# Three float32r products per weight block, or one plain float32 product on two halves of the array

## The chip, the cores and the metric

One core of one Trainium2 chip runs the whole program in one launch. The metric is the device time of an execution in microseconds; the kernel before takes 2727.23 us (median of three runs, 2720.29 to 2727.84). Inputs, outputs and arithmetic are float32.

## The reference

Two layers of a trunk over 512 latent tokens with 256 context tokens in front, width 1024. Each layer is: half-step SwiGLU, token mixing, half-step SwiGLU, each behind an RMS norm modulated by shift and scale from a conditioning vector.

```python
def half_ffn(h, g, shift, scale, gate, w_gu, w_down):
    return h + 0.5 * gate * swiglu(norm_mod(h, g, shift, scale), w_gu, w_down)   # 1024 -> 2 x 2816 -> 1024
# even layer: [windowed GQA with sink | chunked gMLP spatial gating]; odd layer: [multi-scale pooling | 2-D neighbourhood attention]
y = jnp.concatenate([window_gqa(q, k, v, kc, vc, sink), chunk_gmlp(bu, bv, v_gain, ws, bias)], axis=-1) @ w_out
y = jnp.concatenate([multiscale_pool(xp, w_pool, c_scale), neighbourhood_attn(q, k, v, kc, vc, rpb)], axis=-1) @ w_out
```

The context needs no last half step, so three half steps run over 768 tokens and the fourth over 512. The output is the latent stream (1, 512, 1024).

## The kernel before, in words

The stream `h` lies in SBUF with channels on partitions, in 8 chunks of 128 (`KC`), tokens in the free dimension. Tokens come in groups: `XG` (512 latents), `CG` (256 context tokens), and at the end of the odd mixer `X0` and `X1` (256 latents each). A weight block is 128 rows by 128 columns; a dense product takes a block as the stationary operand and 512 or 256 tokens as the moving one. Per half step there are 22 chunks of the inner dimension (`NFF`), each with 8 gate blocks, 8 up blocks and 8 down blocks, so 528 blocks; the even mixer has 112 blocks in and 64 out, the odd one 128 in (64 of them, pool input and queries, for the latents alone) and 64 out.

Every dense operand is split in two float32r parts, high and low. `chain` (L515) and `out_block` (L529) multiply a block in three products: high by high, high by low, low by high. So do the attention scores (`scores`, L1196 and L1563) and the pooling product (`pooling`, L1647). The parts are made by other engines: weights by `Stream` (L354), which loads 512 KB units into three raw tiles on SyncE's queue, copies the high part (`do_split`) and subtracts the low part (`low`); the modulated input by `modulate` (L581, `second` and `third`); the SwiGLU activations by `hilo` (L348); queries and keys by `headnorm` (L1148); the mixers' outputs by their own copies and subtractions.

Some products are plain float32 already: the attention values (`values`, L1249 and L1603), where each key tile is two calls, one per head of a pair, on 64 columns of the array each, with outputs in the two halves of the partitions; the spatial gating (L1301), in the same form; the modulation vectors (`Ada.job`, L716, and `first_mods`, L970), on 32 columns in four ranges; small sums over partitions (`blk2`, `ones`). Transposes by the identity are float32 on all 128 columns.

The order of the work is written out by the program itself. `Machine` and `Engine.cost` (L64, L155) keep a model of the engines' clocks; `Sched` (L198) holds lanes of background steps (attention, softmax, norms, modulation, gating) and `tick`, called after each dense block, emits those whose operands the model says are ready. `wait_for` (L282) emits background steps alone until a condition holds. The half steps run `ffn_plan` (L447): gate and up of each chunk, and after every second chunk the down product of two chunks. The mixers run `EV_PLAN` and `OD_PLAN` (L298, L300).

The lines of `Engine.cost` that price a TensorE product:

```python
if ins[0].dtype == F32R:
    return n / 2.4 + 2.5
# beside a product on the first columns of the array, those on other columns cost little
if Machine.free(ins[0]) < 128:
    return n / 0.6 + 10.0 if out.offset < out.ap[0][0] else 32.0
return max(n / 0.6, 168.0)
```

Of the kernel before, what the change touches and what calls it, by code (L numbers as in the profile page):

```python
# [8 lines left out]
F32R = mybir.dt.float32r  # L9
# [4 lines left out]
D = 1024  # L14
# [15 lines left out]
LEADS = [400.0, 600.0]  # L30

# Shape-only constants, one row of columns per partition.
# [31 lines left out]
class Machine:  # L64
    """The operations on their way to the engines, with a model of the engines' clocks beside them:
    when an engine gets to an operation, and when its result is there. The order of emission rests on it."""

    # from one engine's result to another's start
# [19 lines left out]
    def rows(self, ap):  # L88
        """What is known of the memory behind an access, and the access's extent."""
# [61 lines left out]
class Engine:  # L151
# [3 lines left out]
    def cost(self, eng, op, out, ins):  # L155
# [42 lines left out]
class Sched:  # L198
    """Emits background steps between the dense matrix products, when the model has their operands ready."""
# [51 lines left out]
    def tick(self, lanes="nmstabg", hooks=True):  # L251
# [7 lines left out]
        for _ in range(40):  # L259
            # what is ready first goes first  # L260
# [21 lines left out]
    def wait_for(self, cond):  # L282
        """Background steps alone, until it holds."""
# [12 lines left out]
# The order of the mixers' dense products: projections by their outputs' names, parts of the way out with the parts they  # L296
# take ("o:" all tokens, "x:"/"c:" latents/context, "0:"/"1:" halves of the latents).
# [6 lines left out]
def trunk(ctx, tc, t, out, stop=None, dbg=None):  # L304
# [5 lines left out]
    rawp = ctx.enter_context(tc.tile_pool(name="rawp", bufs=3))  # L310
# [22 lines left out]
    def copy(out, in_):  # L333
        """By the engine that has it done first."""
# [5 lines left out]
    def minus(out, a, b):  # L340
        """By VectorE or GpSimd, which has it done first."""
        n = Machine.free(out)
        if max(nc.t["dve"], sch.now) + 1.04 * n > max(nc.t["pool"], sch.now) + 2.2 * n + 200.0:
            nc.gpsimd.tensor_tensor(out=out, in0=a, in1=b, op=ALU.subtract)
        else:
            nc.vector.tensor_sub(out, a, b)

    def hilo(hi, lo, src):  # L348
        """Two float32r parts; the lower one when VectorE has time."""
        copy(hi, src)  # L350
        sch.later(sch.at([hi], slack=100.0, eng="dve", lead=300.0), lambda: nc.vector.tensor_sub(lo, src, hi.bitcast(F32)))

# [1 line left out]
    class Stream:  # L354
        def __init__(self):
            self.units = []
            self.dma = self.split = self.taken = 0
            self.raw, self.w, self.low = {}, {}, {}
            self.Q, self.ahead = 3, 3
            # (a room, the units from which on it is no longer there)  # L360
            self.free = [([main.tile([128, D], F32R, name=f"w{i}{p}") for p in "hl"], None) for i in range(4)]
            self.ends, self.long, self.upto = {}, set(), None

        def lend(self, rooms, units):
            """More rooms, of use to the next units only."""
            self.free += [(w, self.taken + units) for w in rooms]

        def room(self, i):
            self.free = [f for f in self.free if f[1] is None or i < f[1]]
            # what stays long goes to a lent room, for the others to have the lasting ones  # L370
            lent = [f for f in self.free if (f[1] is not None) == (i in self.long)]
            return (lent or self.free or [None])[0]

        def pump(self):
            while self.dma < (len(self.units) if self.upto is None else self.upto) and self.dma < min([self.split, *self.low]) + self.Q:
                raw = rawp.tile([128, D], F32, tag="raw", name="raw")
                for dst, src in self.units[self.dma]:
                    nc.sync.dma_start(out=dst(raw), in_=src)
                self.raw[self.dma] = raw
                self.dma += 1  # L380
            i = self.split
            if i < self.dma and i < self.taken + self.ahead:
                r = self.room(i)
                if (r is not None and nc.after([self.raw[i]], [r[0][0]]) <= sch.now
                        and min(nc.t["act"], nc.t["dve"]) <= sch.now + 200.0):
                    self.do_split()

        def do_split(self):
            i = self.split
            raw = self.raw.pop(i)  # L390
            r = self.room(i)
            assert r is not None, i
            self.free.remove(r)
            w, self.ends[id(r[0])] = r
            copy(w[0], raw)
            self.w[i] = w
            self.split += 1

            def low():
                if i in self.low:  # L400
                    self.low.pop(i)
                    if max(nc.t["dve"], sch.now) > max(nc.t["pool"], sch.now) + 1500.0:
                        nc.gpsimd.tensor_tensor(out=w[1], in0=raw, in1=w[0].bitcast(F32), op=ALU.subtract)
                    else:
                        nc.vector.tensor_sub(w[1], raw, w[0].bitcast(F32))
            self.low[i] = low
            sch.later(lambda: max(nc.after([w[0]], []), min(nc.t["dve"], nc.t["pool"] + 1500.0) - 200.0), low)

        def take(self):
            i = self.taken  # L410
            self.taken += 1
            self.pump()
            while self.split <= i:
                self.do_split()
                self.pump()
            if i in self.low:
                self.low[i]()
            return self.w.pop(i)

        def release(self, *ws):  # L420
            self.free += [(w, self.ends[id(w)]) for w in ws]
            self.pump()

    stream = Stream()
    sch.hooks.append(stream.pump)
# [5 lines left out]
    def cols2_unit(w, c0, c1):  # L431
        u = []
        for i, c in enumerate((c0, c1)):
            src = w[:, c:c + 64].rearrange("(k p) f -> p k f", p=128)
            u.append((lambda r, i=i: r.rearrange("p (k f) -> p k f", k=KC)[:, :, 64 * i:64 * i + 64], src))
        return u

    def rows_unit(w, r0):
        return [(lambda r: r, w[r0:r0 + 128, :])]

    def rows2_unit(w, r0, r1):
        return [(lambda r: r[0:64], w[r0:r0 + 64, :]), (lambda r: r[64:128], w[r1:r1 + 64, :])]

    DOWN_BLOCKS = [[2 * i, 2 * i + 1] for i in range(NFF // 2)]

    # a block of the down product comes one chunk after its last part is there
    def ffn_plan(both, first=False):  # L447
        plan = []
        for c in range(NFF):
            plan.append(("gu", c))  # L450
            if c >= 2 and c % 2 == 0:
                plan.append(("down", c // 2 - 1))
        if first:
            # for the gate to get ready
            plan[3:5] = plan[4:2:-1]
        plan.append(("down", NFF // 2 - 1))
        if both:
            # the latents run ahead at the end, so that their norm has the context's products to hide behind
# [1349 lines left out]
```

## Time and profile before

| | |
|---|---|
| timed runs, us | 2727.84, 2727.23, 2720.29 |
| span of the profiled execution, us | 2725.2 |
| its time beyond the span | not on the page; the median is 2.0 us above the span |
| PE busy, share of the span | 2655.8 us, 97% |
| DVE, ACT, POOL busy | 1711.8, 744.4, 683.8 us |
| DMA | 249.31 MB, mean 91 GB/s |
| stages, us from the start | first half step to 617, even mixer to 936, two half steps to 2088, odd mixer to 2350, last half step to the end |

Busy time of PE is the union of its matmul records; since matmuls are pipelined, one record lasts longer than the distance to the next start, so pace is read from starts and not from durations. A record is one executed instruction, and one call in the program can be more than one record. PEclk is the granted clock as a share of 2.4 GHz.

### The profile page before, as it was taken

The numbers are of one execution on the slowest core, as the hardware profiler recorded it, in microseconds if no ns is written. First come the engines' busy times: TensorE is split into PE (matmuls) and PEld (weight loads), VectorE is DVE, ScalarE is ACT, GpSimd is POOL, SyncE is SP. The second block draws the span as 40 slices with busy tenths as digits, with TensorE's granted clock in tenths as the row PEclk, the third lists the DMA queues.
The fourth block names the chain that finished last, engine by engine and source line by source line (L and its number), as shares of the span: only waits on it lengthen the run. The fifth ranks groups of instructions, "written<-read, shape, count | busy, mean of one in ns | idle before, by whom it ended". The sixth has DMA issues, their size and how long they took to land.

```text
span 2725.2 us, 37838 instructions
## 1 busy us (share of the span) xinstructions
PE 2655.8 (97%) x15678; PEld 2284.7 (84%) x15678; DVE 1711.8 (63%) x2459; ACT 744.4 (27%) x1195; POOL 683.8 (25%) x440
## 2 busy tenths in 40 slices
PE   7999999999999889999999999999999999899999
PEld 5888888888888778888888888888888887888887
DVE  6787885456676677788784545444456657644554
ACT  4332331124434432323321411111114333311111
POOL 2453540013433333434440200000003443200000
PEclk9999999999999899999999999999999999899999
DMA  9443532222111144434432122222221212133332
GB/s 271 141 147 124 160 127 62 70 55 72 32 42 34 31 147 147 147 125 145 152 114 70 39 63 64 66 61 74 63 62 52 69 47 64 59 99 93 93 93 85
DMA packets 286918, 249.31 MB, mean 91 GB/s; under 512 B 26178, under 2 KB 256026, under 8 KB 286746
## 3 DMA queue, kind: packets, MB, share of 16 engines
q1 hardware_dynamic: 286378, 246.81, 30.1%
q8 instruction: 123, 2.02, 0.3%
q14 instruction: 49, 0.40, 0.0%
q10 hardware_dynamic: 176, 0.07, 0.0%
q0 software_dynamic: 192, 0.01, 0.0%
HBM read 244.73 MB, written 2.13 MB: 91 GB/s over the span
## 4 chain that ended last, share of the span: by engine, by line
PE 90%; DVE 5%; issue 2%; ACT 1%; POOL 1%; DMA 1%; SPq 0%; ACTq 0%; DVEq 0%; POOLq 0%
PE gb L194 47%; PE bank_c L194 13%; PE bank_d L194 13%; PE bank_e L194 9%; PE bank_f L194 3%; PE S L194 2%; DVE a L194 1%; PE Sx L194 1%; DVE zl L194 1%; PE TB L194 1%; POOL aacc L194 0%; DVE h L194 0%; DMA araw<-in_ada_w 0%; DVE w L194 0%; DMA alent<-in_ada_w 0%
## 5 line engine op out<-in xcount | busy, mean ns | idle before, releaser
L194 DVE TENSOR_TENSOR a<-sg,gb 128x512 f32<-128x512 f32 (+1 forms) x151 | 85.7, 567 | 522.0 <-PE gb L194 521.5
L194 POOL TENSOR_TENSOR aacc<-aacc,amul 128x1024 f32<-128x1024 f32 x112 | 303.6, 2711 | 308.0 <-ACT amul L194 308.0
L194 DVE SCALAR_TENSOR_TENSOR aacc<-araw,st,aacc 128x1024 f32<-128x1024 f32 x112 | 230.8, 2061 | 3.4 <-DMA araw<-in_ada_w 1.5
L194 POOL TENSOR_TENSOR acc<-acc,sq 128x512 f32<-128x512 f32 (+1 forms) x24 | 25.8, 1075 | 780.4 <-ACT sq L194 779.2
L194 PE MATMUL gb<-zl,w0h 128*128 128x512 f32 (+1 forms) x600 | 207.0, 345 | 3.3 <-DVE zl L194 3.2
L194 PE MATMUL gb<-zh,w1h 128*128 128x512 f32 (+1 forms) x608 | 210.1, 346 | 0.0
L194 PE MATMUL gb<-zl,w1h 128*128 128x512 f32 (+1 forms) x608 | 209.0, 344 | 0.0
L194 PE MATMUL gb<-zh,w1l 128*128 128x512 f32 (+1 forms) x608 | 208.8, 343 | 0.0
L194 PE MATMUL gb<-zh,w0h 128*128 128x512 f32 (+1 forms) x600 | 207.9, 347 | 0.0
L194 PE MATMUL gb<-zh,w0l 128*128 128x512 f32 (+1 forms) x600 | 206.2, 344 | 0.0
L194 ACT CAST a<-a 128x512 fp32r<-128x512 f32 (+1 forms) x152 | 80.2, 527 | 460.7 <-DVE a L194 460.4
L194 DVE SCALAR_TENSOR_TENSOR h<-bank_c,mod,h 128x512 f32<-128x512 f32 (+1 forms) x240 | 152.3, 635 | 72.3 <-PE bank_c L194 72.3
L194 PE MATMUL gb<-zh,w3h 128*128 128x512 f32 (+1 forms) x576 | 197.7, 343 | 0.0
L194 PE MATMUL gb<-zl,w3h 128*128 128x512 f32 (+1 forms) x576 | 197.3, 343 | 0.0
L194 PE MATMUL gb<-zh,w3l 128*128 128x512 f32 (+1 forms) x576 | 197.2, 342 | 0.0
L194 DVE SCALAR_TENSOR_TENSOR h<-bank_d,mod,h 128x512 f32<-128x512 f32 (+1 forms) x237 | 150.5, 635 | 70.4 <-PE bank_d L194 70.0
L194 ACT ACTIVATE sg<-gb 128x512 f32<-128x512 f32 (+1 forms) x151 | 75.6, 500 | 418.7 <-PE gb L194 418.7
L194 PE MATMUL gb<-zh,w2h 128*128 128x512 f32 (+1 forms) x536 | 185.1, 345 | 0.0
L194 PE MATMUL gb<-zl,w2h 128*128 128x512 f32 (+1 forms) x536 | 184.1, 344 | 0.0
L194 PE MATMUL gb<-zh,w2l 128*128 128x512 f32 (+1 forms) x536 | 184.0, 343 | 0.0
L194 ACT ACTIVATE amul<-araw,st 128x1024 f32<-128x1024 f32 x112 | 128.8, 1150 | 149.8 <-POOL aacc L194 128.5
L194 DVE TENSOR_TENSOR a<-a,a 128x512 fp32r<-128x512 f32 (+1 forms) x156 | 126.7, 819 | 43.9 <-ACT a L194 43.7
(558 smaller groups left out, 6758.7 us busy)
## 6 DMA issues: line engine op xcount, KB each, us to landing
raw<-in_ffn_w_gu SPq DMA_DIRECT2D x176, 512.0 KB, 4.6
araw<-in_ada_w SPq DMA_DIRECT2D x134, 512.0 KB, 4.0
raw<-in_ffn_w_down SPq DMA_DIRECT2D x88, 512.0 KB, 3.8
raw<-in_od_w_in SPq DMA_DIRECT2D x16, 512.0 KB, 4.1
raw<-in_ev_w_in SPq DMA_DIRECT2D x10, 512.0 KB, 3.7
raw<-in_od_w_out SPq DMA_DIRECT2D x8, 512.0 KB, 3.6
xt<-in_ada_w SPq DMA_DIRECT2D x6, 512.0 KB, 7.2
xt<-in_x SPq DMA_DIRECT2D x4, 512.0 KB, 5.3
```

The source lines that it names most:

```text
L194: return real(*args, **kw)
```

## The change

All float32r parts go. The modulated input is one tile `z`, the SwiGLU activations one value per element, queries and keys `qf` and `kf`, the mixer's slots plain float32 tiles. A dense block is multiplied by `mm`: two plain float32 products, on the first and the last 64 columns of the block, with outputs in the two halves of the partitions and the same moving operand. The scores and the pooling product go the same way. `Stream` loads 1 MB units (two chunks' columns, or two row blocks) straight into seven rooms, with no raw tile and no split. The down product takes four chunks at a time in place of two. `Engine.cost` has other prices for products. The plans of the mixers, `ADA_GAP`, softmax, values, spatial gating and the modulation vectors stay as they are.

```diff
-            if ins[0].dtype == F32R:
-                return n / 2.4 + 2.5
-            # beside a product on the first columns of the array, those on other columns cost little
             if Machine.free(ins[0]) < 128:
-                return n / 0.6 + 10.0 if out.offset < out.ap[0][0] else 32.0
-            return max(n / 0.6, 168.0)
+                return n / 1.2 + 4.0 if out.offset < out.ap[0][0] else 6.0
+            return max(n / 0.6, 112.0)
...
+    def mm(ps, w, z, start, stop):
+
+        for x in range(2):
+            wx = w[x] if isinstance(w, tuple) else w[:, 64 * x:64 * x + 64]
+            nc.tensor.matmul(ps[64 * x:64 * x + 64], wx, z, start=start, stop=stop)
...
     def cols_unit(w, c0):
-        src = w[:, c0:c0 + 128].rearrange("(k p) f -> p k f", p=128)
-        return [(lambda r: r.rearrange("p (k f) -> p k f", k=KC), src)]
+        return [(by_k, w[:, c0:c0 + 256].rearrange("(k p) f -> p k f", p=128))]
...
-            wh, wl = [p[:, 128 * k:128 * k + 128] for p in w]
-            zs = slice(t0, t0 + n)
-            nc.tensor.matmul(ps, wh, zh[:, k, zs], start=(k == 0), stop=False)
-            nc.tensor.matmul(ps, wh, zl[:, k, zs], start=False, stop=False)
-            nc.tensor.matmul(ps, wl, zh[:, k, zs], start=False, stop=(k == KC - 1))
+            mm(ps, w[k], z[:, k, t0:t0 + n], k == 0, k == KC - 1)
             sch.tick()
...
-                        wh, wl = [p[:, 128 * d:128 * d + 128] for p in units[i]]
-                        nc.tensor.matmul(room[d], wh, slots[i][:, 0, zs], start=(i == 0), stop=False)
-                        nc.tensor.matmul(room[d], wh, slots[i][:, 1, zs], start=False, stop=False)
-                        nc.tensor.matmul(room[d], wl, slots[i][:, 0, zs], start=False, stop=(i == nb - 1))
+                        mm(room[d], units[i][:, 128 * d:128 * d + 128], slots[i][:, zs], i == 0, i == nb - 1)
...
-            nc.vector.tensor_tensor(out=a32, in0=sg, in1=ru, op=ALU.mult)
-            hilo(a[:, 0, ts], a[:, 1, ts], a32)
+            nc.vector.tensor_tensor(out=a, in0=sg, in1=ru, op=ALU.mult)
...
-                    for qa, ka in ((0, 0), (0, 1), (1, 0)):
-                        nc.tensor.matmul(S[:, o:o + n], q[rows, qa, qs], khl[rows, ka, kk:kk + n],
-                                         start=(qa + ka == 0), stop=(qa == 1))
+                    mm(S[:, o:o + n], q[rows, qs], kf[rows, kk:kk + n], True, True)
```

## Rows read from the trace of the kernel before

**Rows 1.** The page, part 1: busy time, share of the span, instructions.
```profile
PE 2655.8 (97%) x15678; PEld 2284.7 (84%) x15678; DVE 1711.8 (63%) x2459; ACT 744.4 (27%) x1195; POOL 683.8 (25%) x440
```
**Rows 2.** The chain that ended last, shares of the span by line.
```profile
PE gb L194 47%; PE bank_c L194 13%; PE bank_d L194 13%; PE bank_e L194 9%; PE bank_f L194 3%; PE S L194 2%; DVE a L194 1%; PE Sx L194 1%; DVE zl L194 1%; PE TB L194 1%; POOL aacc L194 0%; DVE h L194 0%; DMA araw<-in_ada_w 0%; DVE w L194 0%; DMA alent<-in_ada_w 0%
```
**Rows 3.** Windows, PE alone: stretch, busy (records), granted clock, DMA share, GB/s.
```profile
1599.37:1649.35 49.98, 49.98 (x289) 1.00 0.22 64
```
**Rows 4.** Timeline of PE, dense products: start, us, instruction, rows*columns, output.
```profile
1650.80 0.39 PE L194 MATMUL gb<-zl,w3h 128*128 128x512 f32 x1
...
1651.93 0.39 PE L194 MATMUL gb<-zh,w3h 128*128 128x512 f32 x1
...
1660.68 0.28 PE L194 MATMUL gb<-zh,w3l 128*128 128x256 f32 x1
...
1661.88 0.28 PE L194 MATMUL gb<-zh,w3h 128*128 128x256 f32 x1
```
**Rows 5.** The odd mixer's value products: the group, and their stretches on the timeline.
```profile
L194 PE MATMUL bank_f<-opT,ovnat 128*64 128x128 f32 x256 | 17.9, 280 | 0.0
...
2143.47 1.09 PE L194 MATMUL bank_f<-opT,ovnat 128*64 128x128 f32 x16
2144.50 0.39 PE L194 MATMUL bank_d<-zh,w1h 128*128 128x256 f32 x1
...
2167.55 0.44 PE L194 MATMUL bank_f<-opT,ovnat 128*64 128x128 f32 x4
2167.92 1.05 PE L194 MATMUL bank_e<-blk,w 128*128 128x2 f32 x8
2168.90 0.88 PE L194 MATMUL bank_f<-opT,ovnat 128*64 128x128 f32 x12
2169.71 0.39 PE L194 MATMUL bank_d<-zh,w3h 128*128 128x256 f32 x1
```
**Rows 6.** The modulation products on 32 columns: the group, and one stretch by start.
```profile
L194 PE MATMUL bank_f<-aacc,pick 128*32 128x256 f32 x256 | 18.0, 401 | 7.3 <-issue 7.3
...
98.22 0.61 PE L194 MATMUL bank_f<-aacc,pick 128*32 128x256 f32 x8
...
98.66 0.40 PE L194 MATMUL bank_f<-aacc,pick 128*32 128x256 f32 x4
```
**Rows 7.** The scores of one item and head: a stretch on the timeline.
```profile
2165.74 0.97 PE L194 MATMUL Sx<-okhl,oqhl 64*128 64x256 f32 x6
2166.64 0.39 PE L194 MATMUL bank_d<-zh,w3h 128*128 128x256 f32 x1
```
**Rows 8.** Transposes on all columns: one group, and two stretches on the timeline.
```profile
L194 PE MATMUL TB<-ident,p 128*128 128x128 f32 x128 | 19.9, 278 | 0.7 <-POOL p L194 0.7
...
2142.89 0.66 PE L194 MATMUL bank_e<-ident,rwx 128*128 128x128 f32 x4
...
2144.96 0.49 PE L194 MATMUL bank_e<-ident,rwx 128*128 128x128 f32 x3
2145.20 0.36 PE L194 MATMUL bank_d<-zh,w1h 128*128 128x256 f32 x1
```
**Rows 9.** What PE waited for: us in total, times, longest us.
```profile
PE bank_c L194 <- DVE zl L194: 5.1, 5, 1.7
PE gb L194 <- ACT a L194: 5.0, 3, 1.7
...
PE bank_c L194 <- DVE h L194: 4.5, 3, 1.8
PE bank_d L194 <- DVE h L194: 4.0, 4, 1.6
```
**Rows 10.** Windows of the mixers: stretch, busy (instructions) of PE, PEld, DVE, ACT, POOL.
```profile
616.80:936.20 319.40, 309.78 (x2108) 258.85 (x2107) 213.96 (x450) 126.94 (x260) 110.91 (x107) 0.99 0.15 40
2088.20:2350.20 262.00, 253.45 (x1653) 212.25 (x1652) 169.05 (x362) 93.33 (x193) 106.66 (x110) 0.99 0.21 58
```
**Rows 11.** One of the four groups that make the weights' low parts on VectorE.
```profile
L194 DVE TENSOR_TENSOR w0l<-raw,w0h 128x1024 fp32r<-128x1024 f32 x72 | 105.3, 1462 | 0.4
```

More of the change, by code (lines that the diff above doesn't have):

```diff
@@ L354, in trunk @@
     class Stream:
         def __init__(self):
[L356 to L372, printed above, removed]
-        def pump(self):
[L375 to L379, printed above, removed]
-                self.dma += 1
[L381 to L407, printed above, removed]
@@ L409, in take @@
-        def take(self):
-            i = self.taken
-            self.taken += 1
-            self.pump()
-            while self.split <= i:
-                self.do_split()
-                self.pump()
[L416 to L422, printed above, removed]
-    stream = Stream()
-    sch.hooks.append(stream.pump)
+            self.keys, self.dmas, self.uses, self.rooms = [], {}, {}, {}
@@ new lines, in __init__, with plan @@
+            self.dma = 0
+            self.free = [main.tile([128, 2 * D], F32, name=f"w{i}") for i in range(ROOMS)]
+            self.upto = None
+        def plan(self, key, dmas):
+            if key not in self.uses:
+                self.keys.append(key)
+                self.dmas[key], self.uses[key] = dmas, 0
+            self.uses[key] += 1
+        def pump(self):
+            while self.free and self.dma < (len(self.keys) if self.upto is None else self.upto):
+                room = min(self.free, key=lambda r: nc.after([], [r]))
+                self.free = [r for r in self.free if r is not room]
+                key = self.keys[self.dma]
+                for dst, src in self.dmas[key]:
+                    nc.sync.dma_start(out=dst(room), in_=src)
+                self.rooms[key] = room
+                self.dma += 1
@@ new lines, in there, with get, release, by_k @@
+        def there(self, key):
+            return key in self.rooms
+        def get(self, key):
+            self.pump()
+            assert key in self.rooms, key
+            return self.rooms[key]
+        def release(self, key):
+            self.uses[key] -= 1
+            if not self.uses[key]:
+                self.free.append(self.rooms.pop(key))
+                self.pump()
+    stream = Stream()
+    def by_k(r):
+        return r.rearrange("p (k f) -> p k f", k=KC)
+    def part(r, i):
+        return [by_k(r)[:, k, 128 * i:128 * i + 128] for k in range(KC)]
@@ L436, in cols2_unit @@
-        return u
[L438 to L447, printed above, removed]
+        for i, rs in enumerate(rows):
+            n = 128 // len(rs)
+            for x, r0 in enumerate(rs):
+                u.append((lambda r, i=i, x=x, n=n: r[n * x:n * x + n, D * i:D * i + D], w[r0:r0 + n, :]))
@@ L448, in ffn_plan @@
+        return u
+    BLOCKS = [list(range(i, min(i + 4, NFF))) for i in range(0, NFF, 4)]
+    def ffn_plan(both):
         plan = []
@@ L450, in ffn_plan @@
             plan.append(("gu", c))
[L451 to L456, printed above, removed]
+            if c >= 4 and c % 4 == 0:
+                plan.append(("down", c // 4 - 1))
+        plan.append(("down", len(BLOCKS) - 1))
         if both:
-            a, b, d = NFF - 2, NFF - 1, NFF // 2 - 1
+            a, b, d = NFF - 2, NFF - 1, len(BLOCKS) - 1
             plan[-4:] = [("gux", a), ("down", d - 1), ("gux", b), ("downx", d), ("guc", a), ("guc", b), ("downc", d)]
@@ new lines, in mixer_units @@
+        for s in plan:
+            if s[1:2] == ":":
+                rows = []
+                for x in s[2:].split(","):
+                    j = int(x[1])
+                    if even:
+                        rows.append((64 * j, 64 * j + 256) if x[0] == "a" else (512 + 128 * j,))
+                    else:
+                        rows.append(((512 if x[0] == "a" else 0) + 128 * j,))
+                stream.plan(("e" if even else "o", s[2:]), parts_unit(w_out, rows))
+                continue
+            for x in s.split(","):
+                key, i = mix_key(even, x)
+                if key[1] == "kv":
+                    u = cols_unit(w_in, 512)
+                elif even and key[1] == "q":
+                    u = cols2_unit(w_in, 128 * key[2], 128 * key[2] + 256)
+                elif even:
+                    u = cols_unit(w_in, {"bu": 768, "bv": 1280}[key[1]] + 256 * key[2])
+                else:
+                    u = cols_unit(w_in, {"p": 0, "q": 512, "k": 1024, "v": 1536}[key[1]] + 256 * key[2])
+                stream.plan(key, u)
@@ L502, in trunk, with weights @@
+    def weights(even, s):
+        key, i = mix_key(even, s)
+        r = stream.get(key)
+        return halves(r, i) if even and key[1] == "q" else part(r, i)
     ffn_units(0, 0)
@@ L527, in soonest, with out_block @@
         return min(banks, key=lambda b: nc.after([], [b]))[:, 0:n]
-    def out_block(slots, units, li, vec, groups, banks, final=None, release=True, quiet=False, ready=None):
+    def out_block(slots, units, li, vec, groups, banks, final=None, quiet=False, ready=None):
         nb, step = len(slots), len(banks) - 1
@@ L794, in gu @@
                 chain(ru, wu, grp)
-            nc.vector.tensor_tensor(out=a32, in0=sg, in1=ru, op=ALU.mult)
-            hilo(a[:, 0, ts], a[:, 1, ts], a32)
-        both, kept, cd = len(groups) == 2, {}, (bank_c, bank_d)
-        plan = ffn_plan(both, (li, fi) == (0, 0))
+            nc.vector.tensor_tensor(out=a, in0=sg, in1=ru, op=ALU.mult)
+        both, cd = len(groups) == 2, (bank_c, bank_d)
+        plan = ffn_plan(both)
         if early is not None:
@@ L826, in ffn, with gu_weights, gu_release, ffn_early @@
                     sch.wait_for(lambda: sch.done(gated))
-                if kind in ("down", "downx"):
-                    us = [stream.take() for _ in DOWN_BLOCKS[i]]
-                part = {"down": groups, "downx": groups[:1], "downc": groups[1:]}[kind]
-                last = i == len(DOWN_BLOCKS) - 1
-                banks = tuple(gb[0:3]) if kind == "downc" else cd + (gb[0], gb[1]) if last else cd + (bank_e,)
-                out_block([slots[cc % 4] for cc in DOWN_BLOCKS[i]], us, li, gate, part, banks, final if last else None,
-                          kind != "downx", not last)
-    def ffn_early(norm, chunks, grps):
-        ws = [(stream.take(), stream.take()) for _ in range(chunks)]
+                us = []
+                for p in BLOCKS[i][::2]:
+                    r = stream.get((li, fi, "d", p))
+                    us += [r[:, 0:D], r[:, D:2 * D]]
+                part_ = {"down": groups, "downx": groups[:1], "downc": groups[1:]}[kind]
+                last = i == len(BLOCKS) - 1
+                banks = tuple(gb[0:3]) if kind == "downc" else cd + (gb[0], gb[1]) if last else cd + (bank_e,)
+                out_block([slots[cc % 6] for cc in BLOCKS[i]], us, li, gate, part_, banks, final if last else None, not last)
+                for p in BLOCKS[i][::2]:
+                    stream.release((li, fi, "d", p))
+    def gu_weights(li, fi, c):
+        return [part(stream.get((li, fi, x, c // 2)), c % 2) for x in "gu"]
+    def gu_release(li, fi, c):
+        for x in "gu":
+            stream.release((li, fi, x, c // 2))
+    def ffn_early(li, fi, norm, chunks, grps):
+        ws = [gu_weights(li, fi, c) for c in range(chunks)]
         n = grps[0][1]
@@ L951, in enter @@
             for b in range(2):
[L952 removed]
+                room = gb[2 + b if i >= 4 else (2 * i + b) % 4]
                 yield sch.at([raw], [room])
@@ L1036, in trunk @@
         sch.add("t", more_loads())
-        zh, zl = [main.tile([128, KC, T], F32R, tag=x, name=x) for x in ("zh", "zl")]
+        z = main.tile([128, KC, T], F32, name="z")
         rooms = {(0, 0): (gb[0], gb[1]), (0, TX): (gb[2][:, 0:TC], gb[3][:, 0:TC]),
@@ L1046, in side_by_side @@
                 sch.tick()
-                if stream.split > len(ws) < 4:
-                    ws.append(stream.take())
+                while len(ws) < 4 and stream.there((0, 0, "gu"[len(ws) % 2], 0)):
+                    ws.append(part(stream.get((0, 0, "gu"[len(ws) % 2], 0)), len(ws) // 2))
                 best, when = None, sch.now + 500.0
@@ L1067, in side_by_side @@
                     sums.remove(best)
-                    for key in ((c, t0), (c, i, "w")):
-                        ends[key] = ends.get(key, 0) + 1
-                    if ends[c, i, "w"] == 2:
-                        stream.release(ws[2 * c + i])
+                    ends[c, t0] = ends.get((c, t0), 0) + 1
                     if ends[c, t0] == 2:
@@ L1074, in side_by_side @@
                         gu(c, None, None, best[3], rooms[c, t0])
+            for c in range(2):
+                gu_release(0, 0, c)
             return 2
@@ L1084, in trunk @@
             return
-        kvq = [stream.take() for _ in range(3)]
+        kvq = [weights(True, x) for x in ("k", "v", "q0")]
         for room, w in zip((bank_c, bank_d, bank_e), kvq):
@@ L1107, in trunk @@
             nc.sync.dma_start(out=gbias[64 * hf:64 * hf + 64], in_=bsrc)
-        slots = [mp.tile([128, 2, T], F32R, name=f"ms{i}") for i in range(4)]
-        khl = mp.tile([128, 2, T], F32R, name="khl")
-        qhl = [mp.tile([128, 2, T], F32R, name=f"qhl{i}") for i in range(2)]
+        slots = [mp.tile([128, T], F32, name=f"ms{i}") for i in range(4)]
+        kf = mp.tile([128, T], F32, name="kf")
+        qf = [mp.tile([128, T], F32, name=f"qf{i}") for i in range(2)]
         vnat = mp.tile([128, 6, 128], F32, name="vnat")
@@ L1132, in kind_of, with proj @@
             return "x" if grp[1] == TX else "c"
-        def proj(w, groups, after, release=True, rooms=(bank_c, bank_d)):
+        def proj(s, groups, after, rooms=(bank_c, bank_d)):
+            w = weights(even, s)
             for grp in groups:
@@ L1162, in headnorm @@
                                   r[:, :2 * nt].rearrange("p (a o) -> p a o", o=1).to_broadcast([128, 2 * nt, 64]))
+            to = dst[:, t0:t0 + n]
+            if not rope:
+                yield from gate(before)
             yield sch.at([rbc[:, :n]], [M])
@@ L1175, in headnorm @@
                 yield sch.at([qn], slack=100.0)
-                nc.vector.tensor_tensor(out=qn, in0=qn, in1=sw, op=ALU.add)
-            yield from gate(before)
-            copy(dst[:, 0, t0:t0 + n], qn)
-            yield sch.at([dst[:, 0, t0:t0 + n]], slack=100.0)
-            nc.vector.tensor_sub(dst[:, 1, t0:t0 + n], qn, dst[:, 0, t0:t0 + n].bitcast(F32))
+                yield from gate(before)
+                nc.vector.tensor_tensor(out=to, in0=qn, in1=sw, op=ALU.add)
         def vtrans(raw, grp):
@@ L1416, in trunk @@
                 vkeep(bank_d, XG)
-                for w, after in zip(kvq, (ak, vkeep, aq)):
-                    proj(w, (CG,), after, rooms=(bank_f, bank_c, bank_d))
+                for x, after in zip(s.split(","), (ak, vkeep, aq)):
+                    proj(x, (CG,), after, rooms=(bank_f, bank_c, bank_d))
             elif s[0] == "q":
                 j = int(s[1])
-                proj(stream.take(), (XG, CG), hkeep(s, V_AQ, qhl[j % 2], "a%d" % (j - 2) if j >= 2 else None))
+                proj(s, (XG, CG), hkeep(s, V_AQ, qf[j % 2], "a%d" % (j - 2) if j >= 2 else None))
             elif s[0] == "b":
                 j = int(s[2])
-                proj(stream.take(), (XG, CG), gate_part(s))
+                proj(s, (XG, CG), gate_part(s))
                 if s[1] == "u":
@@ L1432, in trunk @@
                 sch.wait_for(lambda: parts[-1] in held)
-                if s[0] != "c":
-                    us = {x: stream.take() for x in parts} if s[0] == "o" else {**us, **{x: stream.take() for x in parts}}
                 grps = {"o": (XG, CG), "x": (XG,), "c": (CG,)}[s[0]]
-                out_block([held[x] for x in parts], [us[x] for x in parts], 0, 5, grps,
-                          LAST[s[0]] if s in ends else (bank_c, bank_d), n2 if s in ends else None, s[0] != "x",
+                r = stream.get(("e", s[2:]))
+                out_block([held[x] for x in parts], [r[:, D * i:D * i + D] for i in range(2)], 0, 5, grps,
+                          LAST[s[0]] if s in ends else (bank_c, bank_d), n2 if s in ends else None,
                           ready=lambda: until(parts))
+                stream.release(("e", s[2:]))
                 if s[0] != "x":
@@ L1441, in trunk @@
             if s == last:
-                free.extend(zh[:, 2 * i:2 * i + 2] for i in range(4))
+                free.extend(z[:, i] for i in range(4))
         if stop == "mix0":
@@ L1475, in trunk @@
             return
-        kvq = [stream.take() for _ in range(3)]
+        kvq = [weights(False, x) for x in ("k0", "v0", "q0")]
         for room, w in zip((bank_c, bank_d, bank_e), kvq):
@@ L1639, in attention2 @@
                         pv = PV.rearrange("p (m r c) -> p m r c", m=4, r=8)
-                        dst = [permuted(slot[:, i], "q") for i in range(2)]
-                        nc.scalar.copy(dst[0], pv)
-                        yield sch.at([slot[:, 0]], slack=100.0)
-                        nc.vector.tensor_tensor(out=dst[1], in0=pv, in1=dst[0].bitcast(F32), op=ALU.subtract)
+                        nc.scalar.copy(permuted(slot, "q"), pv)
                         done.add(name)
@@ L1721, in trunk @@
             if s == "k0,v0,q0":
-                ak, av = hkeep2("k0", V_DK, khl[0], "k", CG), vkeep2(0)
-                hkeep2("q0", V_DQ, qhl[0], "q", XG)(bank_e, XG)
+                ak, av = hkeep2("k0", V_DK, kf[0], "k", CG), vkeep2(0)
+                hkeep2("q0", V_DQ, qf[0], "q", XG)(bank_e, XG)
                 ak(bank_c, XG)
                 av(bank_d, XG)
-                stream.release(kvq[2])
-                for w, after in zip(kvq, (ak, av)):
-                    proj(w, (CG,), after, rooms=(bank_f, bank_c, bank_d))
+                stream.release(mix_key(False, "q0")[0])
+                for x, after in zip(s.split(","), (ak, av)):
+                    proj(x, (CG,), after, rooms=(bank_f, bank_c, bank_d))
             elif s[1] == ":":
@@ L1732, in trunk @@
                 sch.wait_for(lambda: parts[-1] in held)
-                if s[0] != "1":
-                    us = {x: stream.take() for x in parts} if s[0] == "o" else {**us, **{x: stream.take() for x in parts}}
                 grps = {"o": (XG,), "0": (X0,), "1": (X1,)}[s[0]]
-                out_block([held[x] for x in parts], [us[x] for x in parts], 1, 5, grps,
-                          LAST[s[0]] if s in ends else (bank_c, bank_d), n5 if s in ends else None, s[0] != "0",
+                r = stream.get(("o", s[2:]))
+                out_block([held[x] for x in parts], [r[:, D * i:D * i + D] for i in range(2)], 1, 5, grps,
+                          LAST[s[0]] if s in ends else (bank_c, bank_d), n5 if s in ends else None,
                           ready=lambda: until(parts))
+                stream.release(("o", s[2:]))
                 if s[0] != "0":
```

201 lines of the change are left out of this document (62 added, 139 removed).

## The prediction

> **What bounds the kernel now.** The page's busy times come first: PE is busy for 2655.8 us of 2725.2, and no other engine for more than 63% [rows 1]. Busy is not yet bound, so the chain of waits comes second: 82% of it is PE at work into `gb`, `bank_c`, `bank_d` and `bank_e`, the rooms of the dense products [rows 2]. Third, a window of the last half step shows what such a stage is made of: 49.98 us for one turn of two chunks, PE busy in all of it, clock granted in full, which is the 2.4 GHz level, DMA at 0.22 [rows 3]. A turn is 48 weight blocks by two groups of tokens in three products, 288 records. So PE's pace sets the time, and DVE, on which most of the splitting lies (one of four such groups: 105.3 us [rows 11]), is beside the path. The question is one of pace: what do three float32r products cost, and what two plain ones on half the columns?
>
> **The old price.** Between 1650.80 and 1651.93 there are five starts at 512 tokens, between 1660.68 and 1661.88 ten at 256 [rows 4]: some 227 and 120 ns. The turn fixes the pair better: 48 x 3 x (a + b) = 49.98 gives a + b = 347.1 ns, so 227.2 and 119.9. A block costs 682 ns at 512 tokens and 360 at 256.
>
> **The new price.** No 64-column product of 512 tokens is in the trace, but the value products have the very form of `mm`: two plain float32 calls on the two column halves, outputs in the two halves of the partitions. Their count is the first thing to read: 4 head pairs x 4 column blocks x 4 key tiles x 2 heads are 128 calls, and the group has 256 records [rows 5]. One call is two records, so a key tile is four. The timeline then gives the time of a tile: four records (one tile) take 0.37 us to the next start, twelve 0.81, sixteen 1.03 [rows 5]. (1.03 - 0.37) / 3 = 0.22 us for each further tile of 128 tokens, and some 0.15 us for each stretch as a whole. That this is a cost per token, and what runs side by side, is told by the modulation products at 256 tokens: 16 vectors x 2 x 4 column ranges are 128 calls, again 256 records [rows 6]; eight records, two for each of the four ranges, go from 98.22 to 98.66 [rows 6]. One after the other, a record would take 55 ns at 128 tokens on two ranges and the same 55 ns at 256 on four, which makes no sense of the tokens; side by side by range, it takes 110 ns at 128 and 220 at 256. Twice the tokens, twice the time: near 0.84 ns a token and record, two cycles of 2.4 GHz, and two records a call. For `mm`: 2 x 216 = 432 ns at 256 tokens, 2 x 429.5 = 859 at 512. Bounds: 853 and 427 with nothing beside the cycles; above, each record carrying the 14 ns by which the float32r records exceed one cycle a token (227.2 against 213.3), 881 and 454. I take 859 and 432, since the rows with this tiling show no such surplus.
>
> The Trainium skill, "TensorE: Matmul & The Clock Gate", section "Back-to-back issue gap", gives N / 2.4 + 2.5 ns for the distance of warm matmuls, 215.8 at 512; the trace has 227.2 for the float32r ones. By the page the old products would be some 145 us cheaper and the change that much dearer; the measurement decides.
>
> **Dense products, the main term.** By the loops: 528 x 4 + 112 + 64 + 128 + 32 less 32 (two chunks' gate and up, last half step, done in halves), and 4 for pooling, are 2420 products of 512 tokens; 528 x 3 + 64 + 112 + 64 + 64 + 64 are 1952 of 256. The change is 2420 x (859 - 682) + 1952 x (432 - 360) = 428 + 141 = +569 us. All of it is on the path, since PE is. Bounds from the prices above: +545 and +666.
>
> **Scores.** 128 parts of 256 tokens and 16 of 384. Now six records, two parts, take 0.90 us with the way in and out [rows 7], 0.45 a part; as pairs 0.43 plus the same way in and out. Together +8 us, between -5 and +20.
>
> **Changes of tiling.** After four transposes, the value products wait: 0.58 us from 2142.89 to 2143.47; three transposes into a dense product of the same 128 columns take 0.24 [rows 8]. So 145 ns against 80 per transpose, or some 0.26 us at the change. The way out of 64 columns costs about 0.1 (of the 0.15 per stretch above). Dense products will now be on 64 columns and the transposes and small sums stay on 128: each stretch of these between dense products pays both. They come in fours to eights (the group of 128 [rows 8] is 32 stretches); over all such groups I count some 150 beside dense products. 150 x 0.27 = 40 us, less some 50 sides of value and gating stretches that become free, 5 us: I take +30, between +10 and +50.
>
> **Splits, waits, loads.** The casts and subtractions go, on DVE, ACT and POOL; they lie under PE, so they save only where PE waited for one. PE's idle time is 69 us in all (2725.2 - 2655.8), of which waits for `zl`, `a` and `h` are the part that a freer DVE shortens, 18.6 us in the four largest rows [rows 9]; more hides under modelled ends, since a turn beside the modulation sums is longer than one without. I take -25, between 0 and -80. Four chunks to a down product halve the updates of `h`, also under PE. The unit loads are the same bytes in fewer, larger transfers on SP's queue, with seven rooms ahead of a slower consumer, against a DMA share of 0.22 [rows 3]: nothing, and at most a few us at the start, where the first unit is 1 MB instead of two halves.
>
> **Order.** The planner's prices fall to n / 1.2 + 10 for a pair, 437 ns at 512, half of what the rows say. Its clock will run ahead: a dense block is thought done early, so background steps come out later among the blocks than the engines could take them. In half steps that is harmless, operands are ready sooner than asked. In the mixers dense blocks run out before attention does, and its last items stand with less beside them. PE is now busy for 309.8 of 319.4 us in the even one and 253.5 of 262.0 in the odd [rows 10]. I take +20, between -5 and +110 (a third of 24 items at some 9 us and of 16 at 7, bare).
>
> **Sum.** 2725.2 + 569 + 8 + 30 - 25 + 20 = 3327 us of span, and the 2 us by which the median exceeds the span: 3330 us, 22% slower.
>
> **Rivals.**
> *One pass per pair* (not slower; in fact much faster): the two records that start together could be the two parts of one call, with a pair then done in one slot, as the new price list has it. Then 512 tokens cost 436 ns and 256 222, dense products fall by 2420 x 0.246 + 1952 x 0.138 = 865 us, and with +30 for tilings and +45 for waits laid bare the time is about 1935 us. It decides below 1.6 slots a pair (682 / 429). For it: records do run side by side, and nothing in the rows says which with which. Against it: counting calls, not records, 0.22 us buys two calls of 128 tokens [rows 5], whichever record is whose. 4%. The Trainium skill, "TensorEngine Tiling", section "Theoretical Speedup", allows up to twice the rate where a dimension is 64 or less; here 128 columns are cut into two 64s, so by that rule only the packing of both halves is won, which the rows show already.
>
> *The surplus stays*: records on 64 columns carry the 14 ns of the float32r ones. 8744 record slots x 11 ns = +97, 3425 us. For it: nobody knows from these rows why 512 x 128 has it. Against: rows 5 and 6. 8%.
>
> *Bare mixers*: the misjudged order costs the +110, 3420 us. For it: the halved prices. Against: PE lags the planner by as much, and later work fills it. 11%.
>
> *All waits go*: the 69 us of idle and what hides under modelled ends shrink by 80 to 100 with the split work, no cost of tilings: 3245 us. 7%.
>
> **How the numbers follow.** 70% for the sum, in 3270 to 3390; the rivals as given. The range 3235 to 3435 holds the sum's own and most of three rivals; what is left out is the first one. Within 0.3% (8 us, about what a measurement of this kernel can tell from no change) would need terms cancelling by chance: 1%. Faster 4%, slower 95%.
>
> **What would show it.** Right: in a half step a turn of two chunks takes 62.0 us (48 x 1.291) in place of 49.98, each block has four records, two at a time, with 430 ns from one two to the next at 512 tokens. PE stays above 95% busy, DVE falls below 40%. The mixers are longer by 80 to 150 us together (their own 81 of the 569, and most of the tilings, scores and order). Wrong: twos at 430 ns with only two records per block, or a turn below 50 us; a granted clock below full would void all prices.

## The result, and the profile after

The changed kernel takes 3395.61 us (median of four runs, 3393.11 to 3395.8) against 2723.98 for the kernel before beside it: ratio 1.246, 95% interval 1.244 to 1.248. The profiled execution's span is 3391.0 us. Forecast: 3330 us, range 3235 to 3435, slower.

The page of the kernel after, part 1 (to set beside [rows 1]), and its chain by line (beside [rows 2]):

```profile
span 3391.0 us, 45131 instructions
...
PE 3247.3 (96%) x20194; PEld 1433.5 (42%) x20194; DVE 796.4 (23%) x1426; ACT 482.3 (14%) x819; POOL 527.0 (16%) x400
...
PE gb L191 50%; PE bank_c L191 15%; PE bank_d L191 13%; PE bank_e L191 10%; PE bank_f L191 3%; PE S L191 2%; POOL aacc L191 2%; PE Sx L191 1%; ACT amul L191 1%; PE TB L191 1%; DVE nm L191 0%; DMA w<-in_ffn_w_gu 0%; DVE S L191 0%; POOL p L191 0%; ACT z L191 0%
```

DVE has lost more than half of its work, from 1711.8 to 796.4 us, and the kernel has become slower by a quarter: DVE was beside the path. PE has two products per block in place of three, and they take longer. Windows of the kernel after, PE alone, each one turn of four chunks (beside [rows 3]), and timeline rows of a down product, blocks of 512 and of 256 tokens (beside [rows 4]):

```profile
2083.46:2207.30 123.84, 123.84 (x771) 1.00 0.16 52
2207.30:2331.14 123.84, 123.84 (x771) 1.00 0.16 52
...
528.02 1.03 PE L191 MATMUL bank_c<-a,w 128*64 128x512 f32 x4
528.88 1.03 PE L191 MATMUL bank_e<-a,w 128*64 128x512 f32 x4
...
555.49 0.60 PE L191 MATMUL bank_d<-a,w 128*64 128x256 f32 x4
555.92 0.60 PE L191 MATMUL bank_c<-a,w 128*64 128x256 f32 x4
```

Two chunks take 61.92 us (half of 123.84), 62.0 were forecast; a block has four records and goes 0.86 us to the next start at 512 tokens, 0.43 at 256. So the price was right to the second digit. What was not forecast is in the waits of PE (columns as in [rows 9]: us in total, times, longest):

```profile
PE bank_f L191 <- DVE aacc L191: 59.2, 4, 20.0
PE bank_f L191 <- POOL aacc L191: 25.0, 3, 8.3
PE S L191 <- POOL p L191: 19.3, 13, 4.5
```

The waits of [rows 9] for `a` and `h` are gone or small; that for `zl` has become one for `z`, 9.0 us. What is new is that PE waits 84.2 us for `aacc`, the sums of the modulation vectors, whose code the change does not touch. Where this is: windows of the kernel after around these waits, up to the next dense product (the second begins with 8 us of dense products), then of the two mixers, from the last product into `gb` before each to the first after it; and the same two mixer stretches of the kernel before.

```profile
1735.40:1806.50 71.10, 8.56 (x58) 0.53 0.37 111
604.50:639.10 34.60, 10.79 (x89) 0.68 0.26 76
```
```profile
778.00:1182.00 404.00, 376.66 (x2558) 0.96 0.11 34
2634.00:2941.60 307.60, 301.23 (x2092) 1.00 0.16 48
```
```profile
622.70:953.80 331.10, 318.66 (x2124) 0.97 0.15 42
2094.20:2366.20 272.00, 262.89 (x1718) 0.97 0.20 57
```

Over 71 us PE works for 8.6, and the granted clock falls to 0.53, near the 1.2 GHz level. The list names DVE first, but what the work hangs on there is GpSimd's additions to `aacc`, 61% of the chain from 1738 to 1800, and ScalarE's products before them, 22%. Both stretches lie just before the third last chunk of the first and of the second half step, at `wait_for(lambda: not sch.lanes["b"])`: there the program empties the lane of the sums before it goes on. The kernel before has the same line and no wait there (its 7.3 us before a product of the sums [rows 6] are at 993.22, early in the second half step). The mixers are longer by 108 us together (80 to 150 were forecast), the even one with 19 us of waits for the scaled softmax `p`.

Two theories for the 64 us above the forecast. *Order*: the planner's halved price spoils the order, in half steps too, which the forecast excluded. *Products*: the change itself costs more than counted (tilings, scores, loads of half-width weights).

### The profile page after: what moved, and what is told of

Its sections match the earlier page's. It is cut to its first block, busy times and chain, and to the rows that moved or that the text cites. A ratio compares the mean times of both kernels' runs of the same rounds, so it can differ in the third digit from the quotient of the medians.

```text
span 3391.0 us, 45131 instructions
## 1 busy us (share of the span) xinstructions
PE 3247.3 (96%) x20194; PEld 1433.5 (42%) x20194; DVE 796.4 (23%) x1426; ACT 482.3 (14%) x819; POOL 527.0 (16%) x400
## 4 chain that ended last, share of the span: by engine, by line
PE 94%; POOL 2%; ACT 1%; DVE 1%; issue 1%; DMA 0%; ACTq 0%; SPq 0%; DVEq 0%; POOLq 0%
PE gb L191 50%; PE bank_c L191 15%; PE bank_d L191 13%; PE bank_e L191 10%; PE bank_f L191 3%; PE S L191 2%; POOL aacc L191 2%; PE Sx L191 1%; ACT amul L191 1%; PE TB L191 1%; DVE nm L191 0%; DMA w<-in_ffn_w_gu 0%; DVE S L191 0%; POOL p L191 0%; ACT z L191 0%
## 5 line engine op out<-in xcount | busy, mean ns | idle before, releaser
L191 PE MATMUL gb<-z,w 128*64 128x512 f32 (+1 forms) x9664 | 1641.5, 500 | 9.6 <-DMA w<-in_ffn_w_gu 6.2
L191 PEld LDWEIGHTS gb<-z,w 128*64 128x64 f32 x9664 | 692.2, 138 | 929.4 <-issue 771.3
L191 PE MATMUL bank_c<-a,w 128*64 128x512 f32 (+1 forms) x1568 | 298.4, 505 | 0.0
L191 PE MATMUL bank_d<-a,w 128*64 128x512 f32 (+1 forms) x1536 | 290.2, 503 | 0.0
L191 PE MATMUL bank_e<-a,w 128*64 128x512 f32 (+1 forms) x1504 | 282.5, 501 | 0.0
L191 PE MATMUL bank_c<-z,w 128*64 128x512 f32 (+1 forms) x976 | 210.4, 555 | 5.7 <-ACT z L191 5.6
L191 PEld LDWEIGHTS bank_c<-a,w 128*64 128x64 f32 x1568 | 111.9, 137 | 156.0 <-issue 131.9
L191 PEld LDWEIGHTS bank_d<-a,w 128*64 128x64 f32 x1536 | 109.7, 137 | 152.2 <-issue 128.5
L191 PEld LDWEIGHTS bank_e<-a,w 128*64 128x64 f32 x1504 | 107.6, 137 | 147.3 <-issue 124.1
L191 PE MATMUL bank_d<-z,w 128*64 128x256 f32 (+1 forms) x976 | 160.4, 461 | 0.0
L191 PE MATMUL bank_f<-aacc,pick 128*32 128x256 f32 x256 | 21.3, 447 | 84.2 <-DVE aacc L191 59.2
```

The costliest lines, as they stand in the source:

```text
L191: return real(*args, **kw)
```

## The experiments

**e1_gap0**: the pauses between the steps of the sums taken away.

```diff
-ADA_GAP = 2500.0
+ADA_GAP = 0.0
```


> The changed kernel with ADA_GAP 0 in place of 2500: the planner may issue the steps of the modulation sums without a pause between them. In the changed kernel PE waits 84.2 us for the last sums (59.2 on DVE, 25.0 on POOL), all just before the chunk at which the program empties the sums' lane. Theory (the order: on the planner's clock, which runs twice as fast as PE, the pauses keep the last sums from being issued until nothing else is left): these waits fall below 10 us and the time from 3391 to about 3300, between 3290 and 3320; the pace of the dense products stays, 61.9 us a turn of two chunks. Rival (the sums' own engines are too slow, 2.5 us on POOL and 1.7 on DVE a step): the waits stay within 15 us of 84 wherever the steps are issued, and the time at 3375 to 3400.

Measured: 3376.98 us, 1.240 [1.239, 1.242]. Waits of PE:

```profile
PE bank_f L191 <- DVE aacc L191: 47.6, 3, 22.2
PE S L191 <- POOL p L191: 17.4, 12, 4.5
PE bank_f L191 <- POOL aacc L191: 14.5, 3, 8.3
```

84.2 became 62.1 us. The time lies in the rival's range, but the waits fit neither side: the pauses are a part, not the cause, and the waits are not of fixed size either.

**e2_prices**: the planner's price alone, near what the chip takes.

```diff
-                return n / 1.2 + 4.0 if out.offset < out.ap[0][0] else 6.0
+                return n / 0.65 + 4.0 if out.offset < out.ap[0][0] else 6.0
```


> The changed kernel with one line of the planner's prices changed: the first product of a pair at n / 0.65 + 4 in place of n / 1.2 + 4, so 798 ns for a pair of 512 tokens (the trace shows 859) in place of 437. ADA_GAP stays 2500. Theory (the halved price spoils the order): the waits for the sums go (84 us) without touching their pauses, and in the mixers the 19 us for the scaled softmax and a few us more; the time about 3280, between 3260 and 3310. Rival (the price does not matter, the 64 us above the forecast lie in the products): 3370 to 3395.

Measured: 3248.47 us, 1.193 [1.191, 1.195], some way below the expected range; 147 us less than the changed kernel by one number that no engine ever sees. Page, the longest waits of PE by name, and windows of a turn and of the two mixers:

```profile
PE 3217.8 (99%) x20194; PEld 1421.5 (44%) x20194; DVE 816.8 (25%) x1426; ACT 487.2 (15%) x820; POOL 540.8 (17%) x400
...
PE bank_c L191 <- DMA cv<-in_c_ctx: 7.0, 1, 7.0
PE gb L191 <- DMA w<-in_ffn_w_gu: 6.9, 2, 5.7
PE bank_c L191 <- ACT z L191: 3.8, 4, 1.5
PE gb L191 <- ACT z L191: 2.6, 2, 2.3
PE S L191 <- POOL p L191: 0.7, 2, 0.4
...
2066.80:2190.64 123.84, 123.84 (x771) 1.00 0.15 52
...
746.90:1108.50 361.60, 358.58 (x2572) 1.00 0.13 37
2488.40:2796.90 308.50, 305.35 (x2106) 1.00 0.16 48
```

No wait for `aacc` is left, the softmax's falls from 19.3 to 0.7, the even mixer goes from 404.0 to 361.6, the odd one stays (307.6 and 308.5), and the turn is the same to the hundredth. The order theory stands, and the engines of the sums are fast enough.

**e5_no_rest**: why e1 failed. The code says that during all but the last down product `finish` ticks with the lanes `n` and `m` alone, so a step of the sums is never issued there; the kernel before has the same rule. GpSimd's timeline of the kernel after shows these rests (idle before, and by whom ended):

```profile
529.91 2.36 POOL L191 TENSOR_TENSOR aacc<-aacc,amul 128x1024 f32<-128x1024 f32 x1 [1.26 <-ACT amul L191]
533.53 2.36 POOL L191 TENSOR_TENSOR aacc<-aacc,amul 128x1024 f32<-128x1024 f32 x1 [1.26 <-ACT amul L191]
578.10 2.37 POOL L191 TENSOR_TENSOR aacc<-aacc,amul 128x1024 f32<-128x1024 f32 x1 [42.21 <-ACT amul L191]
```

The rest from 535.89 to 578.10 takes in most of the down product from 528.02 to 569.30 (it is the one shown above). With prices as in the change, two lines are changed, the rule and how early a step may come:

```diff
-            sch.tick(*(("nm", grp != CG) if quiet else ()))
+            sch.tick()
...
-                yield sch.at(self.raws[:1], eng="dve")
+                yield sch.at(self.raws[:1], eng="dve", lead=1000.0)
```


> The changed kernel with its halved prices kept, and two lines changed: the down products no longer hold back the background lanes other than the norms (tick with all lanes), and a step of the modulation sums may be issued while VectorE is busy for up to 1000 ns. Theory (the sums' steps rest through every down product, a third of PE's time, and PE's time on the planner's clock is half of the chip's; so the last sums are left over and are issued with nothing beside them; the pauses of ADA_GAP were a small part, which is why taking them away gave 22 of 84 us): PE's waits for the sums fall below 12 us, the time from 3391 to 3295 to 3315; what remains above e2_prices (3248) is the even mixer, some 40 us. Rival (ScalarE and GpSimd work a step off too slowly): the waits stay above 40 us, the time above 3350.

Measured: 3307.8 us, 1.213 [1.210, 1.215], inside the expected range. The longest waits, and the even mixer:

```profile
PE S L191 <- POOL p L191: 19.5, 13, 4.5
PE bank_c L191 <- DMA cv<-in_c_ctx: 7.0, 1, 7.0
PE gb L191 <- DMA w<-in_ffn_w_gu: 5.8, 1, 5.8
PE bank_c L191 <- ACT z L191: 5.5, 8, 1.5
...
753.70:1161.00 407.30, 379.94 (x2558) 0.95 0.11 34
```

No wait for `aacc`, and the mixer as long as in the changed kernel: the two places are apart, 88 us for the sums, and for the even mixer some 45 us by its windows (407.3 against 361.6), of 59 that are left to e2_prices. Which of the two lines did it, this run does not tell apart.

**e3_full_columns**: one product on 128 columns in place of two on 64, on the base of e2_prices.

```diff
+        if not isinstance(w, tuple):
+            nc.tensor.matmul(ps, w, z, start=start, stop=stop)
+            return
         for x in range(2):
...
```


> As e2_prices, but each dense block and score part is one plain float32 product on all 128 columns in place of two on 64 (the even queries, whose columns lie apart, stay in two). Theory (four cycles a token in either form, the halves only run side by side): two records a block, 427 ns each at 512 tokens plus what a record on 128 columns carries; with the 14 ns of the float32r records a block costs 881 ns against 859, 454 against 432 at 256, and the kernel is 97 us slower than e2_prices less some 30 us of tiling changes that go: +50 to +90, so about 3350. If the surplus is no matter of the columns: 20 to 40 us faster than e2_prices, about 3250. Rival (the halves are what makes the products dear, by their doubled records or weight loads): 100 us or more faster than e2_prices.

Measured: 3250.58 us, 1.194 [1.192, 1.196], the same as e2_prices within the intervals: neither 50 to 90 us slower nor 20 to 40 faster. The planner's price moved with the form, to 853 ns a block (n / 0.6) from 798, so the two times do not differ by the products alone; the rows of the products do not depend on it. A turn, and two blocks of a down product:

```profile
2075.98:2199.82 123.84, 123.84 (x386) 1.00 0.15 51
...
531.04 1.02 PE L191 MATMUL bank_e<-a,w 128*128 128x512 f32 x2
531.90 1.02 PE L191 MATMUL bank_c<-a,w 128*128 128x512 f32 x2
```

Two records a block in place of four, half as many in the turn, and the very same time. PE is busy for 6.6 us less in all (3211.2) and waits some 10 us more.

**e4_quarters**: four products on 32 columns, on the base of e2_prices.

```diff
+        if not isinstance(w, tuple) and z.ap[0][1] == 128:
+            for x in range(4):
+                nc.tensor.matmul(ps[32 * x:32 * x + 32], w[:, 32 * x:32 * x + 32], z, start=start, stop=stop)
+            return
```


> As e2_prices, but each dense block is four products on 32 columns each, eight records (scores and even queries stay in halves). Theory (records run side by side by column range, whatever their number): four at a time some 6 ns apart, a block of 512 tokens at 859 + 2 x 13 ns at most, the kernel 0 to 110 us slower than e2_prices. Rival (only two run at a time, or the issue of records limits): a block near 1720 ns and a time above 5500 us.

Measured: 3251.77 us, 1.194 [1.192, 1.197], at the low end of the theory's range; the rival is out. Eight records a block, and again the same turn:

```profile
2062.68:2186.52 123.84, 123.84 (x1540) 1.00 0.16 52
...
531.83 1.04 PE L191 MATMUL bank_c<-a,w 128*32 128x512 f32 x8
532.69 1.04 PE L191 MATMUL bank_d<-a,w 128*32 128x512 f32 x8
```

By the starts in the traces, records come in pairs some 7 ns apart in the kernel after and in fours in e4_quarters, one at a time in e3_full_columns, and each time the next come 429 ns later. With one range (e3_full_columns) these 429 ns lie between the two records of one call. So records of different column ranges run side by side, and a range passes the two parts of a call one after the other.

**g1_plain_scores**: in the kernel before, this part of the change alone.

```diff
-                    for qa, ka in ((0, 0), (0, 1), (1, 0)):
-                        nc.tensor.matmul(S[:, o:o + n], q[rows, qa, qs], khl[rows, ka, kk:kk + n],
-                                         start=(qa + ka == 0), stop=(qa == 1))
+                    mm(S[:, o:o + n], q[rows, qs], khl[rows, kk:kk + n])
...
-            copy(dst[:, 0, t0:t0 + n], qn)
-            yield sch.at([dst[:, 0, t0:t0 + n]], slack=100.0)
-            nc.vector.tensor_sub(dst[:, 1, t0:t0 + n], qn, dst[:, 0, t0:t0 + n].bitcast(F32))
...
```


> The kernel before with one part of the change alone: queries and keys stay plain float32, and each score part is two plain products on 64 columns in place of three float32r ones; dense products as before. Theory (a score part costs the same either way, 63 us of e2_prices against 64.8, and what the change takes from DVE is worth something only where PE waits): PE's score stretches stay within 5 us, some 60 casts and subtractions of 0.4 to 0.8 us leave DVE and ACT in the mixers, and the kernel is 0 to 15 us faster, 2708 to 2723. Rival (plain float32 is dear in the scores too, 4 passes against 3): 15 to 25 us slower. Rival (the waits that splitting causes in the mixers are large): more than 20 us faster.

Measured: 2729.45 us against 2725.86, 1.002 [1.001, 1.003] over five rounds: slower by some 4 us, so no theory had it. Page and two waits of PE:

```profile
PE 2658.8 (97%) x15822; PEld 2259.3 (83%) x15822; DVE 1691.8 (62%) x2431; ACT 737.5 (27%) x1179; POOL 682.6 (25%) x440
...
PE S L194 <- POOL p L194: 3.7, 6, 1.1
```

PE is busy for 3 us more, DVE for 20 less, and nothing comes of the 20: in the kernel before, PE's waits in the mixers do not hang on these splits.

## Why the prediction was right, and where it was not

*What bounds the kernel*: right. PE 97% before, 96% after; 915 us of DVE's work fell away, and the kernel is slower all the same.

*The new price* (859 and 432 ns, from counting records against calls and from the time of a key tile): right, 0.86 and 0.43, the turn 61.92 us for 62.0 forecast. The rival of one pass per pair is out: 430 ns would be the distance from block to block, it is 860. The rival in which the surplus of 14 ns stays is out by the same rows; a turn of two chunks would be 64 us.

*Dense products, scores, tilings, waits*: 582 us forecast together (569 + 8 + 30 - 25); with the order mended (e2_prices) the span is 3246.7, 521.5 above that of before, so 60 us less. Each term was too high. This can be read by adding up, in both traces, the distance from each record of PE to the next, less the idle time between them:

| us | before | e2_prices | change | forecast |
|---|---|---|---|---|
| dense products | 2412 | 2957 | +545 | +569 |
| scores | 65 | 63 | -2 | +8 |
| all other products (transposes: 70, 92) | 179 | 198 | +19 | +30 |
| idle (span less busy) | 69 | 29 | -40 | -25 |

The dense products of before stand 59 us above 2420 x 682 + 1952 x 360 ns, those of e2_prices 35 above the new prices: the forecast took the prices of an undisturbed turn for all blocks. What the 59 and the 35 are made of (ways in and out of other products, hidden waits) is not told apart. Tilings do cost something: in e3_full_columns the transposes fall from 92 to 78 us, but scores and attention values rise by 13 and the idle time by 10, so nothing of it is left in the time. Of the -40 not all hangs on the splits: waits of 7.3 us for a product of the sums, 4.8 for `alent` and 4.6 for `wide` stand in the list of before and are 0.2 together in e2_prices, while those for the modulated input go only from 9.3 to 6.4.

*Loads*: "a few us at the start" came out in size, not in cause. PE waits 5 to 9 us at once for a weight unit in all runs with 1 MB units, but not for the first: in the kernel after the first two units are issued at 7.33 and 16.96 us, the next only at 77.41, behind the loads for the modulation vectors, and PE waits for that one until 84.23.

*Order*: this step failed. +20 was forecast, +144 measured (3391.0 - 3246.7 by e2_prices), and the sentence that failed is "In half steps that is harmless, operands are ready sooner than asked". It had in mind dense products that wait for background work. But at one place the program waits for a background lane to be empty, and the planner's half step, with blocks at half price, has too little time before that place: a sum's step is issued only between gate and up products and rests through every down product, so, by the code, the number of steps done goes by the planner's PE time and not by the chip's. The last sums are left over and run with almost nothing beside them, 106 us in two stretches (34.6 + 71.1, of which PE works for 19), and the granted clock falls in them. A price near the chip's (e2_prices) or steps in the rests, issued earlier (e5_no_rest), each take these waits away. That the pauses were the cause was a second error, in the expectation of e1_gap0. The even mixer's part, 42 us, was inside what the forecast named (up to 110 for both mixers). It also made the sign of mixers longer by 80 to 150 us come true: without it (e2_prices) the mixers are 67 us longer than before, less than the 81 of their own products. The rival *bare mixers* had the mechanism and the size (3420), but in the wrong place for two thirds of it.

So the sum was 64 us of span low: 124 too little for the order, 60 too much for the rest. That the time lies inside the range is in part luck: with the other terms as forecast, the order alone would have put it at 3330 + 124 = 3454, outside.

## What to carry to other kernels

Before a new form of product is priced, count the records of a call in rows of the same form and read the time per call, at two sizes; here the new price list has a pair at 437 ns where the chip takes 859, half, and the trace of before showed it. Cutting a full block of plain float32 into column ranges won nothing by itself: the ranges only share the pass that the whole block takes. And where an order of work is planned by a model, a wrong price of the bounding engine is paid at each place that waits for a lane to empty: look for these, and for stretches in which the lane may not run.

## What the hardware showed that was not expected

Plain float32 takes 429 ns per record of 512 tokens on 32, 64 and 128 columns alike, with 1540, 771 or 386 records in the same 123.84 us; neither the number of records nor the width of the weight loads shows. So the 14 ns a record by which the float32r products of the kernel before exceed one cycle a token [rows 4] are not a matter of 128 columns as such; what they are stays open.
